# The last two output-gate units of the first mixer, computed as a pair of seven half-size products

## The chip, the cores and the metric

The kernel runs on one core of one Trainium2 chip. TensorE (PE) multiplies, VectorE (DVE), ScalarE (ACT) and GpSimd (POOL) work element by element, and SyncE (SP) and POOL issue DMA transfers. The metric is the device time of one execution in microseconds; the span is the time from the first instruction that the profile shows to the last.

## The reference, cut to what matters

A decoder block over 16 meta tokens and 512 tokens of width 1024, in float32. The normalised input is projected by one wide matrix; two token mixers (an mLSTM, "m", and gated linear attention, "g", four heads each) work on the projections, two branches are merged by sigmoid gates, and a SwiGLU layer follows.

```python
xn = rmsnorm(h, norm1_g[l])
proj = jnp.where(valid, xn @ w_in[l].astype(dt), 0.0).astype(dt)
(mq, mk, mv, mi, mf, mo, gq, gk, gv, ga, gr, gate_m, gate_g) = split_cols(proj)
...
hm = mlstm_chunkwise(...)
hm = head_rmsnorm(from_chunks(hm), m_head_g[l]) * jax.nn.sigmoid(mo.astype(f32)).reshape(bsz, tp, M_HEADS, M_DV)
y_m = hm.reshape(bsz, tp, M_V).astype(dt)
...
merged = (jax.nn.sigmoid(gate_m) * (y_m @ w_branch_m[l].astype(dt))
          + jax.nn.sigmoid(gate_g) * (y_g @ w_branch_g[l].astype(dt)))
h = h + merged @ w_out[l].astype(dt)
```

The change is in how `mo`, the output gates of the mLSTM, are computed for its last head.

## The kernel before, in words

**Units.** A projection is computed transposed, in units of 128 output features: eight blocks k of 128 input features, and for each block three matmuls, since every float32 operand is split into a high part and a low remainder (high x high, high x low, low x high; `mm3`, lines 340 to 347). A unit over the tokens alone is 24 matmuls of 512 columns (`unit_real`); one over all 528 positions is 48 of 264 (`unit_all`). Unit `mo i` gives 128 gate features; head h uses mo 2h and mo 2h+1, `mv` gives the values, `mq` and `mk` queries and keys.

**Pairs.** From the gm units on, two neighbouring units are computed together by a Strassen-like scheme (`pair`, line 397; `seven`, line 384): inputs and columns are halved, and seven products of half size (q1, p7, p3, q6, p4, p2, q5) take the place of eight. Each is four blocks k of three matmuls with 256 or 272 columns. The products share three PSUM banks: bx takes q1, then q6, q5 and p3; bz takes p7 and p4; by takes p2. Between them parts of the banks are copied out by ACT (`s1`, `s2`, `s5`, `s7`, `c12`, lines 475 to 480) and combined by DVE (`c11`, `c21`, `c22`). p3 of one pair, and its last combinations, are computed in the place for p3 of the next pair; the first pair finds that place empty, and takes q1 ahead of p7.

**Weights.** A raw weight tile of each unit arrives on SP's queue, several units ahead (`load_raw`). A plain unit's is split by a cast on ACT and a subtraction on DVE (`split_hi`, `split_lo`). A pair's two tiles are combined: the second gets a half of the first added by an accumulating DMA on POOL; two more halves are fetched as tile `wf` (`fetch_mix`, lines 233 to 245, one pair ahead); DVE adds two halves (`s2` at line 263, `s4` at line 275), and four sets are split: e, a, f and the half-size g. f's low part is made at the end of p7 (`f_lo`), g's parts in q6 and p4.

**Operands.** The first units work on the gained but not yet normalised input `xh`, `xl`, and their results are multiplied by `rstd` when they leave PSUM. `normed_x` (line 629) builds the normalised set block by block, and writes it and negated halves to DRAM (`X.pos`, `X.neg`); when it is done, later units use it and their results are copied out by ACT. `mixed_x` (line 651, once for each half of the blocks) then builds the operands of the seven products: those of p2 and p3 are slices of the normalised set, those of q5, p7, q6 and p4 are read from DRAM with accumulating DMAs on POOL and then split, and those of q1 are copied by SP into tiles of their own (line 707). `X.ready` counts finished halves, and the first pair starts when it is 2.

**Order.** No scheduler reorders anything: the order in which the program is written is the order in each engine's list, and each engine works through its own list, waiting on semaphores. The main list of jobs (`job_list`) gives the matmuls. Everything else is written as Python generators: `tick()` advances each one step, and `yield n` means that its next step comes n ticks later. A unit ticks after each of its eight blocks k, a pair after every second hook, 14 times in all, four of them (two ticks) in the place of p3 even if no p3 is there. The generators in `side` advance on every tick; of `mixers` (the `mlstm` and `gla` heads, in order) only the first one does, so a head begins on the tick after the one before it ended. A head's `mlstm` writes score matmuls (line 1023), its numerators (lines 1076 to 1080, two halves one or two ticks apart) and the denominator (lines 1083 and 1084) in between the matmuls of the units.

The units around the change are, in order: mq 3, mk 3, mv 6, mv 7, mo 6, mo 7, then the pairs gm 0/1 and gm 2/3, then the pairs of the second mixer. `conv_act` (line 838) is the activation of queries and keys, `gates_of` applies tanh to the gates, `head_out` normalises a head's result and multiplies in the gate, `some_parts` splits the first branch operands.

Of the kernel before, what the change touches and what calls it, by code (L numbers as in the profile page):

```python
# [54 lines left out]
def job_list():  # L55

    one = lambda *a: [(x,) for x in a]
    o = one(("gates", 0))
    for h in range(H):
        v, g = [("mv", 2 * h), ("mv", 2 * h + 1)], [("mo", 2 * h), ("mo", 2 * h + 1)]  # L60
        o += one(("mq", h), ("mk", h), *([g[0], *v, g[1]] if h == 0 else v + g))
    two = lambda n, i: [((n, 2 * i), (n, 2 * i + 1))]
    g = lambda h: [(("gq", h), ("gk", h))] + two("gv", h) + two("gr", h)
    bm = lambda i: one(("bm", 2 * i), ("bm", 2 * i + 1))
    bgs = [m for i in range(4) for m in (i, i + 4)]
    o += two("gm", 0) + two("gm", 1) + g(0) + two("gm", 2) + two("gm", 3)
    for i in range(4):
        o += bm(i)
    q, v, r = ([g(h)[i] for h in range(H)] for i in range(3))
    o += [q[1], v[1], q[2], r[1], v[2], q[3], v[3], r[2], r[3]]  # L70
    for i in range(4):
        o += two("gg", i)
    o += one(*(("bg", m) for m in bgs))
    for i in range(4):
        o += two("out", i)
    for m in range(FT):
        if m == 0:
            for i in range(len(GCHUNKS)):
                o += one(("fx", i))
        if m >= NG:  # L80
            o += [(("fg", m), ("fu", m))]
    for i in range(len(CHUNKS)):
        o += one(("down", i))
    return o
# [36 lines left out]
def hybrid_block(ctx: ExitStack, tc: tile.TileContext, xT, xr, wst, wdn, wgu, fg, par, con, out):  # L121
# [14 lines left out]
    def tt(dt=F32, n=NT, p=P):  # L136
        t = tpool.tile([P, TW], dt, tag="t", name=nm("t"))
        return t[:p, :n]
# [34 lines left out]
    def tick():  # L173
        for e in list(side):
            advance(side, e)
        if mixers:
            advance(mixers, mixers[0])
# [452 lines left out]
    def normed_x():  # L630

        nh, nl = [], []
        for k in range(KT):
            t = tt()
            V.scalar_tensor_tensor(t, xs[k], pr[:, C_N1 + k:C_N1 + k + 1], rstd, ALU.mult, ALU.mult)
            yield 4
            hi, lo = tt(F32R), tt(F32R)
            S.copy(hi, t)
            neg = tt(n=HA)
            act(neg, t[:, 256:] if k < 4 else t[:, :HA], AF.Copy, scale=-1.0)  # L640
            nc.sync.dma_start(X.pos[k // 2][k % 2], t)
            nc.sync.dma_start(X.neg[k // 2][k % 2], neg)
            yield 1
            V.tensor_tensor(lo, t, hi.bitcast(F32), ALU.subtract)
            nh.append(hi)
            nl.append(lo)
            yield 2
        X.h, X.l, X.scale = nh, nl, None

    def mixed_x(i):  # L650

        while X.scale is not None:
            yield 24
        h, l = X.h, X.l
        c1, c2 = slice(0, HA), slice(256, NT)
        if X.w is None:
            X.w = {n: ([None] * 4, [None] * 4) for n in SEVEN}
        ks = (2 * i, 2 * i + 1)
        for j in range(2):
            for k in ks:  # L660
                X.w["p2"][j][k] = (h, l)[j][k + 4][:, c1]
                X.w["p3"][j][k] = (h, l)[j][k + 4][:, c2]
        three = lambda a: a.rearrange("p (j n) -> p j n", j=2)
        mem = lambda t, c: t[:, :, c].rearrange("j p n -> p j n")

        def two(n, src, neg=False):
            hi, lo = tt(F32R, 2 * HA), tt(F32R, 2 * HA)
            if neg:
                act(hi, src, AF.Copy, scale=-1.0)
            else:  # L670
                S.copy(hi, src)
            yield 3
            if neg:
                V.scalar_tensor_tensor(lo, src, -1.0, hi.bitcast(F32), ALU.mult, ALU.subtract)
            else:
                V.tensor_tensor(lo, src, hi.bitcast(F32), ALU.subtract)
            for j in range(2):
                for k in ks:
                    X.w[n][j][k] = (hi, lo)[j][:, (k % 2) * HA:(k % 2 + 1) * HA]

        t1, t3 = tt(n=2 * HA), tt(n=2 * HA)
        plus = lambda t, m, c: G.dma_start(three(t), mem(m, c), accum_op=ALU.add)
        nc.sync.dma_start(three(t1), mem(X.pos[i], c1))
        nc.sync.dma_start(three(t3), mem(X.pos[i + 2], c2))
        yield 7
        plus(t1, X.neg[i], c1)
        plus(t3, X.neg[i], c1)
        yield 7
        yield from two("q5", t1)
        yield 1  # L690
        plus(t1, X.pos[i + 2], c2)
        yield from two("p7", t3)
        del t3
        yield 14
        yield from two("q6", t1, True)
        yield 2
        plus(t1, X.neg[i + 2], c1)
        yield 11
        yield from two("p4", t1)
        del t1  # L700
        while unit_ix[0] < UNITS.index(("mo", 7)):
            yield 1
        for j in range(2):
            t = tt(F32R, 2 * HA)
            for k in ks:
                c = slice((k % 2) * HA, (k % 2 + 1) * HA)
                nc.sync.dma_start(t[:, c].bitcast(F32), (h, l)[j][k][:, c1].bitcast(F32))
                X.w["q1"][j][k] = t[:, c]
            yield 5
        X.ready += 1  # L710

    def evac(o, ps):

# [9 lines left out]
    def evac_all(box, ps):  # L723
        t = tt()
        evac(t, ps)
        box.v = t
        yield 1

    def evac_real(box, ps):
        t = tt(n=NS)  # L730
# [114 lines left out]
    def conv_act(q, k, src):  # L845
        while src[0].v is None or src[1].v is None:
            yield 1
        yield 4
        for b, a in ((q, src[0].v), (k, src[1].v)):
            t = tt(n=a.shape[1])  # L850
            act(t, a, AF.Tanh, scale=0.5)
            V.scalar_tensor_tensor(a, t, 1.0, a, ALU.add, ALU.mult)
            del t
        yield 2
        for b, a in ((q, src[0].v), (k, src[1].v)):
            n = a.shape[1]
            hi, lo = tt(F32R, n), tt(F32R, n)
            act(hi, a, AF.Copy, scale=0.5)
            yield 3
            V.scalar_tensor_tensor(lo, a, 0.5, hi.bitcast(F32), ALU.mult, ALU.subtract)  # L860
            b.v = hi, lo, a
        src[0].v = src[1].v = None
# [108 lines left out]
    def part(y, k, j):  # L971

        if j == 0:
            hi = hpool[0].tile([P, NS], F32R, tag="h", name=nm("h")) if k < 6 and y is ym else tt(F32R, NS)
            S.copy(hi, y[k])  # L975
            y[k] = y[k], hi
        else:
            s, hi = y[k]
            lo = tt(F32R, NS)
            V.tensor_tensor(lo, s, hi.bitcast(F32), ALU.subtract)  # L980
            y[k] = hi, lo, True

    def some_parts(y, n):
        if y is ym:
            while y[7] is None:
                yield 5
            open_hpool()
        for k in range(n):
            while y[k] is None:
                yield 7  # L990
            part(y, k, 0)
            yield 3
            part(y, k, 1)
            yield 5

    def mlstm(h, q, k, v, gates, dst):
        while not gts.ready or q.v is None or k.v is None:
            yield 2
        (qh, ql, qf), (kh, kl, kf) = q.v, k.v
        nml, em = tt(n=NS), tt(n=NS)  # L1000
        for t, row in ((nml, 0), (em, 1)):
# [96 lines left out]
    def gla_decay(h, gq, gk, dk):  # L1098
# [14 lines left out]
        for a in range(2):  # L1113
            c = slice(a * HALF, (a + 1) * HALF)
            act(l[:, c], ps[a], AF.Abs, bias=b)
            act(z[:, c], ps[a], AF.Relu, scale=-1.0, bias=nb)
        yield 2
        act(l, l, AF.Exp, scale=-1.0)
        yield 2
        act(l, l, AF.Ln, bias=b_one)  # L1120
# [12 lines left out]
        yield 5  # L1133
        e1, e2 = tt(n=NS), tt()
        act(e2, b3, AF.Exp, scale=1.0 / TAU)
        yield 3
        act(e1, b3[:, NM:], AF.Exp, scale=-1.0 / TAU)
        act(ex[:, 2], b3[:, NM - 1:NT - CH:CH], AF.Exp, scale=-1.0 / TAU)
        while gq.v is None or gk.v is None:
# [7 lines left out]

    def gla(h, dk, v, gates, dst):
        while dk.v is None:
            yield 7  # L1150
        yield 10
        qd, ki, ex = dk.v
        pk = bank()
# [258 lines left out]
    for job in JOBS[2:]:  # L1412
# [3 lines left out]
        if what in ("bm", "bg") and i % 2 or len(job) == 2 or job in JOBS[3:8]:  # L1416
            next(sums, None)
        if len(job) == 2:
            if what == "gm" and i == 0:
                while X.ready < 2:  # L1420
                    tick()
                for k in range(4):
                    X.h[k] = X.l[k] = None
            if what in ("gq", "gv", "gr"):
                b = head("g", i if what == "gq" else i // 2)
            if what == "gq":
                pair(job, X.w, ALL, sink_of((b.q, b.k), False, True))
            elif what == "gv":
                pair(job, X.w, ALL, sink_of(b.vf, True, True))
            elif what == "gr":  # L1430
                pair(job, X.w, REAL, sink_of(b.gates, False, False, AF.Silu))
            else:
                if what == "gg" and i == 6:
                    run(some_parts(yg, 2))
                elif what == "gm" and i == 4:
                    run(some_parts(ym, 4))
                pair(job, X.w, REAL, sink_of({"gm": gm, "gg": gg}[what][i:i + 2], False, False, AF.Tanh))
# [660 lines left out]
```

## Time and profile before

| | before |
|---|---|
| median of 3 runs | 895.92 us (895.58 to 896.02) |
| the profiled execution | 895.85 us |
| its span | 894.1 us |
| PE busy | 883.3 us, 99% |
| DVE busy | 706.7 us, 79% |
| ACT busy | 582.8 us, 65% |
| POOL busy | 115.3 us, 13% |
| HBM | 170.30 MB read, 36.85 MB written |

A row of the timeline gives start and duration in microseconds, engine, line, operation, the tiles written and read, their shapes, the count where rows were merged, and in brackets the idle time before and what ended it. A row of the waits gives the waiting instruction, what it waited for, the microseconds in total, how often, and the longest. A table by windows gives for each stretch its length, each engine's busy time with the number of instructions, TensorE's granted clock, the busy share of the DMA engines and what they moved. A row of groups gives the count, busy time and mean nanoseconds. mo 6 and mo 7 run from 159.71 to 176.11 us, among parts of heads 2 and 3; the first gm pair starts at 176.11.

### The profile page before, as it was taken

What the parts mean: (1) busy time and instruction counts of PE and PEld (TensorE: products, weight loads), DVE (VectorE), ACT (ScalarE), POOL (GpSimd) and SP (SyncE); (2) the same over time, 40 slices, a digit from 0 to 9 for tenths busy, and PEclk for the clock granted to TensorE, in tenths of its full rate; (3) what the DMA queues carried; (4) which work ended last, traced back from release to release, by engine and by line L of the source; (5) the groups of instructions that cost most, each with busy time, mean ns of one, the idle gap of its engine ahead of it and who ended that gap; (6) DMA issues with size and microseconds to landing.
All of it is one profiled execution on the core that took longest, in us unless ns stands there. A gap on an engine that the chain in (4) does not pass through costs nothing. (4 is left out here: it accounts for less than half of the span.)

```text
span 894.1 us, 16395 instructions
## 1 busy us (share of the span) xinstructions
PE 883.3 (99%) x6281; PEld 829.6 (93%) x6281; DVE 706.7 (79%) x1102; ACT 582.8 (65%) x1027; POOL 115.3 (13%) x148
## 2 busy tenths in 40 slices
PE   9999999999999999999999999999999999999996
PEld 8999989889998899999998899999999999988885
DVE  4879776888765477687788899999777777798987
ACT  7677777798774276776876457765655555666564
POOL 0100031022211122221210111011111121000000
PEclk9999999999999999999999999999999999999999
DMA  9887585589985898988978776667877677456562
GB/s 342 269 241 208 155 171 124 162 246 226 247 218 146 210 225 244 251 214 218 227 187 244 198 170 171 210 191 169 198 179 208 178 169 193 122 191 198 179 199 105
DMA packets 67582, 178.93 MB, mean 200 GB/s; under 512 B 7432, under 2 KB 12680, under 8 KB 65072
## 3 DMA queue, kind: packets, MB, share of 16 engines
q1 hardware_dynamic: 50224, 137.07, 46.2%
q0 software_dynamic: 17136, 40.77, 27.7%
q8 instruction: 49, 0.80, 0.4%
q14 instruction: 29, 0.24, 0.1%
q10 hardware_dynamic: 144, 0.04, 0.0%
HBM read 170.30 MB, written 36.85 MB: 232 GB/s over the span
## 5 line engine op out<-in xcount | busy, mean ns | idle before, releaser
L392 PE MATMUL b<-t,whi 128*128 128x256 f32 (+1 forms) x1008 | 289.3, 287 | 2.7 <-ACT t L475 1.8
L226 DVE TENSOR_TENSOR wlo<-raw,whi 128x1024 fp32r<-128x1024 f32 x179 | 214.5, 1200 | 89.3 <-ACT whi L221 88.4
L394 PE MATMUL b<-t,wlo 128*128 128x256 f32 (+1 forms) x1008 | 284.3, 282 | 0.0
L393 PE MATMUL b<-t,whi 128*128 128x256 f32 (+1 forms) x1008 | 284.3, 282 | 0.0
L221 ACT CAST whi<-raw 128x1024 fp32r<-128x1024 f32 x179 | 184.8, 1034 | 42.2 <-PE b L346 9.9
L392 PEld LDWEIGHTS b<-t,whi 128*128 128x128 f32 x1008 | 190.1, 189 | 4.6 <-ACT t L475 2.4
L393 PEld LDWEIGHTS b<-t,whi 128*128 128x128 f32 x1008 | 190.2, 189 | 0.4
L394 PEld LDWEIGHTS b<-t,wlo 128*128 128x128 f32 x1008 | 189.8, 188 | 0.0
L346 PE MATMUL b<-t,whi 128*128 128x264 f32 (+2 forms) x448 | 148.0, 330 | 0.2 <-DVE t L980 0.2
L152 ACT ACTIVATE t<-t 128x512 f32<-128x512 f32 (+10 forms) x168 | 88.2, 539 | 83.8 <-DVE t L1689 39.5
L345 PE MATMUL b<-t,whi 128*128 128x264 f32 (+2 forms) x400 | 131.5, 329 | 0.0
L347 PE MATMUL b<-t,wlo 128*128 128x264 f32 (+2 forms) x400 | 129.5, 324 | 0.2 <-DVE wlo L561 0.2
L346 PEld LDWEIGHTS b<-t,whi 128*128 128x128 f32 x448 | 84.3, 188 | 8.4 <-DVE t L980 0.5
L209 POOL DMA_DIRECT2D raw<-wst x41 | 35.8, 873 | 383.3 <-DMA wf<-wst 108.9
L347 PEld LDWEIGHTS b<-t,wlo 128*128 128x128 f32 x400 | 75.2, 188 | 6.6 <-DVE wlo L561 0.4
L345 PEld LDWEIGHTS b<-t,whi 128*128 128x128 f32 x400 | 75.4, 188 | 6.2 <-ACT t L975 0.2
L1945 PE MATMUL b<-whi,t 128*128 128x512 f32 (+1 forms) x156 | 61.2, 392 | 0.0
L1944 PE MATMUL b<-wlo,t 128*128 128x512 f32 (+1 forms) x156 | 61.2, 392 | 0.0
L1943 PE MATMUL b<-whi,t 128*128 128x512 f32 (+1 forms) x156 | 60.7, 389 | 0.0
L221 ACT CAST whi<-wf 128x1024 fp32r<-128x1024 f32 x42 | 44.1, 1049 | 20.8 <-PE b L393 9.3
L245 POOL DMA_DIRECT2D wf<-wst x42 | 40.2, 963 | 131.4 <-DVE t L1718 35.6
L226 DVE TENSOR_TENSOR wlo<-wf,whi 128x1024 fp32r<-128x1024 f32 x42 | 51.1, 1218 | 0.0
(301 smaller groups left out, 1646.3 us busy)
## 6 DMA issues: line engine op xcount, KB each, us to landing
raw<-wst SPq DMA_DIRECT2D x123, 512.0 KB, 5.0
wf<-wst SPq DMA_DIRECT2D x42, 256.0 KB, 3.9
wf<-wst POOLq DMA_DIRECT2D x42, 256.0 KB, 6.2
raw<-wst POOLq DMA_DIRECT2D x41, 256.0 KB, 4.6
raw<-wdn SPq DMA_DIRECT2D x15, 512.0 KB, 3.7
sum_q<-wdn POOLq DMA_DIRECT2D x10, 512.0 KB, 9.1
sum_p<-wdn POOLq DMA_DIRECT2D x10, 512.0 KB, 9.0
raw<-sum_q SPq DMA_DIRECT2D x10, 512.0 KB, 4.1
```

The source lines that it names most:

```text
L152: S.activation(o, i, func, **kw)
L221: S.copy(t, src)
L226: V.tensor_tensor(t, src, hi.bitcast(F32), ALU.subtract)
L345: T.matmul(o, w_h, ah[:, c0:c1], start=first, stop=False)
L346: T.matmul(o, w_h, al[:, c0:c1], start=False, stop=False)
L347: T.matmul(o, w_l, ah[:, c0:c1], start=False, stop=last)
L392: T.matmul(o, h, xh_[k][:, c0:c1], start=start and k == 0, stop=False, skip_group_check=not start)
L393: T.matmul(o, h, xl_[k][:, c0:c1], start=False, stop=False, skip_group_check=not start)
L394: T.matmul(o, l, xh_[k][:, c0:c1], start=False, stop=k == 3, skip_group_check=not start)
L1943: T.matmul(o, hi, wh, start=n not in INTO and k == 0 or (i, k) == (1, FH - 2), stop=False, skip_group_check=True)
L1944: T.matmul(o, hi, wl, start=False, stop=False, skip_group_check=True)
L1945: T.matmul(o, lo, wh, start=False, stop=k == FH - 1, skip_group_check=True)
```

## The change

mo 6 and mo 7 become one job, `two("mo", 3)`, ahead of the gm pairs: the first pair of the kernel. Its sink applies tanh to the combined result as before. q1's operands are slices of the normalised set while that pair runs, and are copied into tiles of their own while it runs: one of the two `mixed_x` generators makes all four copies, from the first tick behind mv 7 on. The wait for `X.ready` stands ahead of every pair. The set `normed_x` takes ten ticks a block instead of seven. In `mixed_x` one step comes a tick sooner. Further steps get other tick counts: `conv_act`, `mlstm` (polls on every tick), `gla_decay`, `gla` and `some_parts`, which also skips a part that is already split; `evac_all` has another count at its very end.

```diff
@@ job_list
-        o += one(("mq", h), ("mk", h), *([g[0], *v, g[1]] if h == 0 else v + g))
+        o += one(("mq", h), ("mk", h), *([g[0], *v, g[1]] if h == 0 else v + g if h < 3 else v))
     two = lambda n, i: [((n, 2 * i), (n, 2 * i + 1))]
+    o += two("mo", 3)
@@ normed_x
             nc.sync.dma_start(X.neg[k // 2][k % 2], neg)
-            yield 1
+            yield 4
             V.tensor_tensor(lo, t, hi.bitcast(F32), ALU.subtract)
@@ mixed_x
                 X.w["p3"][j][k] = (h, l)[j][k + 4][:, c2]
+                X.w["q1"][j][k] = (h, l)[j][k][:, c1]
...
         plus(t3, X.neg[i], c1)
-        yield 7
+        yield 6
...
-        while unit_ix[0] < UNITS.index(("mo", 7)):
-            yield 1
-        for j in range(2):
-            t = tt(F32R, 2 * HA)
-            for k in ks:
-                c = slice((k % 2) * HA, (k % 2 + 1) * HA)
-                nc.sync.dma_start(t[:, c].bitcast(F32), (h, l)[j][k][:, c1].bitcast(F32))
-                X.w["q1"][j][k] = t[:, c]
-            yield 5
         X.ready += 1
+        if X.ready < 2:
+            return
+        while unit_ix[0] <= UNITS.index(("mv", 7)):
+            yield 1
+        for k in range(0, 4, 2):
+            for j in range(2):
+                t = tt(F32R, 2 * HA)
+                for m in range(2):
+                    c = slice(m * HA, (m + 1) * HA)
+                    nc.sync.dma_start(t[:, c].bitcast(F32), X.w["q1"][j][k + m].bitcast(F32))
+                    X.w["q1"][j][k + m] = t[:, c]
+                    (h, l)[j][k + m] = None
+                yield 2
@@ conv_act
-        yield 2
+        yield 3
         for b, a in ((q, src[0].v), (k, src[1].v)):
...
-            yield 3
+            yield 2
@@ mlstm
         while not gts.ready or q.v is None or k.v is None:
-            yield 2
+            yield 1
@@ gla_decay
-        yield 2
+        yield 1
         act(l, l, AF.Exp, scale=-1.0)
...
-        yield 3
+        yield 5
         act(e1, b3[:, NM:], AF.Exp, scale=-1.0 / TAU)
@@ gla
-            yield 7
+            yield 8
@@ some_parts
-            part(y, k, 0)
-            yield 3
-            part(y, k, 1)
+            if not isinstance(y[k], tuple):
+                part(y, k, 0)
+            yield 4
+            if len(y[k]) == 2:
+                part(y, k, 1)
@@ main loop, jobs of two units
-            if what == "gm" and i == 0:
-                while X.ready < 2:
-                    tick()
-                for k in range(4):
-                    X.h[k] = X.l[k] = None
+            while X.ready < 2:
+                tick()
...
+            elif what == "mo":
+                pair(job, X.w, REAL, sink_of(head("m", i // 2).gates, False, False, AF.Tanh))
```

More of the change, by code (lines that the diff above doesn't have):

```diff
@@ L700, in mixed_x @@
         del t1
-        while unit_ix[0] < UNITS.index(("mo", 7)):
+        X.ready += 1
+        if X.ready < 2:
+            return
+        while unit_ix[0] <= UNITS.index(("mv", 7)):
             yield 1
-        for j in range(2):
-            t = tt(F32R, 2 * HA)
-            for k in ks:
-                c = slice((k % 2) * HA, (k % 2 + 1) * HA)
-                nc.sync.dma_start(t[:, c].bitcast(F32), (h, l)[j][k][:, c1].bitcast(F32))
-                X.w["q1"][j][k] = t[:, c]
-            yield 5
-        X.ready += 1
+        for k in range(0, 4, 2):
[7 more added lines that the diff above has]
+                yield 2
     def evac(o, ps):
@@ L853, in conv_act @@
             del t
-        yield 2
+        yield 3
         for b, a in ((q, src[0].v), (k, src[1].v)):
```

## The prediction

> **What bounds the kernel now.** First the page, then the waits of TensorE, then busy time by stretch around the two units.
>
> ```profile
> span 894.1 us, 16395 instructions
> PE 883.3 (99%) x6281; PEld 829.6 (93%) x6281; DVE 706.7 (79%) x1102; ACT 582.8 (65%) x1027; POOL 115.3 (13%) x148
> ```
>
> ```profile
> PE b L392 <- ACT t L475: 1.8, 2, 1.4
> ...
> PE b L392 <- ACT t L476: 0.4, 1, 0.4
> ...
> ```
>
> ```profile
> core 0: us, PE busy (x) PEld busy (x) DVE busy (x) ACT busy (x) POOL busy (x), PEclk, DMA share, GB/s
> 100.00:146.70 46.70, 46.70 (x324) 43.79 (x323) 33.27 (x53) 35.26 (x73) 7.36 (x6) 1.00 0.61 151
> 146.70:159.71 13.01, 13.01 (x107) 12.93 (x106) 10.67 (x22) 10.30 (x21) 3.38 (x3) 1.00 0.56 105
> 159.71:176.11 16.40, 16.40 (x85) 13.87 (x84) 13.52 (x21) 10.59 (x18) 1.71 (x2) 1.00 0.76 209
> 176.11:187.07 10.96, 10.96 (x89) 10.74 (x87) 8.80 (x13) 10.55 (x24) 1.50 (x3) 1.00 0.66 241
> 187.07:199.66 12.59, 10.76 (x90) 10.46 (x89) 10.24 (x21) 10.97 (x22) 3.67 (x5) 1.00 0.92 210
> ```
>
> TensorE sets the time: it is idle for 10.8 us in all, at the granted clock 1.00 here. The last four stretches are mv 6 and mv 7; mo 6 and mo 7, the units that become a pair; the first gm pair; the second gm pair. Only the last has a hole, 1.83 us, and the waits name it: a product that must add to a bank waits until ScalarE has copied that bank out (lines 475 and 476). DVE and ACT are near their limit there, with 2.35 and 1.62 us idle. So the time moves by TensorE's instruction time, plus any new place where it waits for ACT or DVE, less the waits that go.
>
> **The products.** Two units are 2 x 8 x 3 = 48 matmuls of 512 columns; the pair is 7 x 4 x 3 = 84 of 256 columns. What counts is the step from start to start, since a matmul's duration overlaps the next one.
>
> ```profile
> 171.60 0.40 PE L345 MATMUL b<-t,whi 128*128 128x512 f32 x1
> ...
> 174.85 0.39 PE L347 MATMUL b<-t,wlo 128*128 128x512 f32 x1
> ```
>
> ```profile
> 195.10 0.28 PE L392 MATMUL b<-t,whi 128*128 128x256 f32 x1
> ...
> 197.44 0.28 PE L394 MATMUL b<-t,wlo 128*128 128x256 f32 x1
> ```
>
> The first two are 14 steps apart, 3.25 / 14 = 0.2321 us. The others are 20 apart, 2.34 / 20 = 0.1170. So 48 x 0.2321 = 11.14 us go and 84 x 0.1170 = 9.83 come: -1.31 us, all on the path, because TensorE has no hole there.
>
> A rule speaks against this. The Trainium skill (TensorE: Matmul & The Clock Gate, "Back-to-back issue gap") gives about 81 ns a matmul at 128 columns and 131 ns at 512 for a sustained stream with weight loads; an estimate between them for 256 is 98 ns, and by it the change would cost 84 x 98 - 48 x 131 ns = +1.9 us. This case's steps differ from it: 232 and 117 ns, so half the columns cost half the time.
>
> **The side work.** The raw weights of both units were split before (one cast, one subtraction each), and still are. The pair adds a third split of their sum and a fourth of half size, two sums, and the copying out of three banks by parts.
>
> ```profile
> L226 DVE TENSOR_TENSOR wlo<-wf,whi 128x1024 fp32r<-128x1024 f32 x2 | 2.4, 1216 | 0.0
> L295 DVE TENSOR_TENSOR wgl<-wg,wgh 128x512 fp32r<-128x512 f32 x2 | 1.4, 686 | 0.0
> L290 ACT CAST wgh<-wg 128x512 fp32r<-128x512 f32 x2 | 1.2, 623 | 0.0
> L221 ACT CAST whi<-wf 128x1024 fp32r<-128x1024 f32 x1 | 1.1, 1052 | 0.1
> L481 DVE SCALAR_TENSOR_TENSOR t<-b,t 128x256 f32<-128x256 f32 x2 | 0.8, 422 | 0.0
> L475 ACT COPY t<-b 128x256 f32<-128x256 f32 x2 | 0.7, 364 | 0.0
> ```
>
> DVE: 1.22 + 0.69 + two sums of 512 columns, at line 295's 0.69 each, + three combinations at 0.42 = 4.6 us. ACT: 1.05 + 0.62 + five copies at 0.36 = 3.5 us; the two tanh stay. Over 146.70 to 187.07 (40.37 us) the stretches show DVE idle 7.4 us and ACT 8.9 us, so it fits by volume and costs nothing by volume; without that cover it would cost up to 4.6 us. What can cost is its order.
>
> **The new pair's place.** It is the first pair, so no earlier product p3 is pending: q1 and p7 come, then q6 adds to q1's bank at once. q6 needs two late things: the bank copied out (line 475), and the low half of the summed weights, which DVE is told to make only at the end of p7. Each engine works through its own list in order.
>
> ```profile
> 159.71 0.39 PE L345 MATMUL b<-t,whi 128*128 128x512 f32 x1
> ...
> 162.49 0.49 PE L879 MATMUL b<-pr,t 128*128 128x128 f32 x3
> 162.73 0.48 PE L345 MATMUL b<-t,whi 128*128 128x512 f32 x1
> ...
> 164.21 0.40 PE L1078 MATMUL b<-wh,t 128*128 128x512 f32 x1
> ...
> 166.22 0.48 PE L345 MATMUL b<-t,whi 128*128 128x512 f32 x1
> ...
> 166.99 0.39 PE L1083 MATMUL b<-t,onesr 128*128 128x512 f32 x1
> ...
> 167.46 0.39 PE L345 MATMUL b<-t,whi 128*128 128x512 f32 x1
> ```
>
> ```profile
> 162.14 1.06 ACT L221 CAST whi<-raw 128x1024 fp32r<-128x1024 f32 x1
> 163.22 1.28 ACT L151 ACT_TABLE_LOAD   x1
> 164.52 1.17 ACT L152 ACTIVATE t<-t 128x512 f32<-128x512 f32 x2
> ```
>
> ```profile
> 163.50 0.68 DVE L1066 TENSOR_TENSOR t<-t,t 128x512 fp32r<-128x512 f32 x1
> 165.18 1.31 DVE L852 SCALAR_TENSOR_TENSOR t<-t,t 128x512 f32<-128x512 f32 x2 [1.00 <-ACT t L152]
> ```
>
> TensorE starts the pair at 159.71; q1 and p7 are 24 x 0.117 = 2.81 us, to 162.52; the transposes of the fourth tick 0.24, to 162.76. Head 2's numerator (2.01 us) and denominator (0.47) now stand on ticks 6 and 7. Head 0 polls every tick instead of every second one, starts a tick sooner, and each head starts when the one before it ends; so I take them on ticks 5 and 6, which in this pair lie in the empty place of p3, ahead of q6. That carries TensorE to 165.24, and the third matmul of q6 comes at 165.5.
>
> On ACT the cast of 162.14 belongs to the pair behind and slides back, so the table load and tanh end about 1.06 us sooner, at 164.6, and the bank is copied by 165.3 (two copies). That is about in time. On DVE the low half stands behind the two operations of line 852, which wait for that tanh: they would end at 166.49 - 1.06 = 165.4, and the subtraction (1.22) at 166.6. One more sum now stands ahead of them; if DVE and not the tanh is last (164.18 + 0.6), it is 167.3. The wait of q6 is so 1.1 to 1.8 us; I take 1.1, since head 2's earlier tick also moves its subtractions out of the way. Its ends: nothing, if both halves of the numerator come first; 167.7 - 162.8 = 4.9 us, if neither does and the tanh is as late as now.
>
> **The old waits.**
>
> ```profile
> 192.02 0.43 DVE L1036 TENSOR_TENSOR t<-b,t 128x272 f32<-128x272 f32 x1
> ...
> ```
>
> ```profile
> 192.49 0.42 ACT L1049 CAST wh<-t 128x272 fp32r<-128x272 f32 x1 [0.97 <-DVE t L1036]
> 192.81 0.37 ACT L475 COPY t<-b 128x256 f32<-128x256 f32 x1
> ```
>
> ```profile
> 193.23 0.38 PE L392 MATMUL b<-t,whi 128*128 128x256 f32 x1 [1.40 <-ACT t L475]
> ...
> 198.16 0.39 PE L392 MATMUL b<-t,whi 128*128 128x256 f32 x1 [0.44 <-ACT t L476]
> ```
>
> Behind the copy stands a cast for head 3, and behind that DVE. Head 3 and the gm pairs keep their places to each other (both come two ticks sooner: the pair has 14 ticks, the units had 16). But the new pair's p3, 12 x 0.117 = 1.40 us of TensorE, is done inside the first gm pair, whose extra work on DVE is one combination (0.42). So DVE has 1.0 us more to catch up. I take 1.0 of the 1.84 us back; the ends are 0 and 1.84.
>
> **What is moved.** The copy of q1's operands is eight SP transfers, now at 161.3 to 167.0:
>
> ```profile
> 161.31 5.71 SPq L707 DMA_DIRECT2D t<-t  x8
> ```
>
> ```profile
> pos<-t SPq DMA_DIRECT2D x5, 264.0 KB, 3.7
> t<-t SPq DMA_DIRECT2D x8, 136.0 KB, 3.3
> ```
>
> They are issued on ticks 1, 3, 5 and 7 of the pair, nearly the same moments, with the same weight loads of SP behind them; they land in 3.3 us and their reader, q1 of the gm pair, is over 8 us away. A pair's weights also need an accumulation on POOL and one more pair of quarter loads, at DMA shares of 0.56 to 0.76. All zero; if SP were held up, the weight loads behind would be, and they run units ahead.
>
> The normalised operands come 24 ticks later (ten ticks a block instead of seven). That puts six bank copies of mk 2, mv 4 and mv 5 on DVE instead of ACT, about 0.4 us each by line 481; DVE idles 13.4 us in 100 to 146.7. The mixed operands are read on the very tick on which the set is complete; its last write went out six ticks (some 4.2 us, at 3 x 0.2321 us a tick) before and lands in 3.7. If that is late, SP waits about a microsecond, then POOL's additions, then the split of q5, which has ticks to spare. Zero, with an end of +1. The other shifted ticks are zero with ends of -0.3 and +0.3.
>
> **Sum.** -1.31 + 1.1 - 1.0 = -1.2 us. The profiled execution took 895.85 us, 1.75 more than its span; the median is 895.92. So 894.7.
>
> **Rivals.** Each time is 895.92 plus the sum. A run here tells from no change only what is over 0.2%, 1.8 us.
>
> *Everything is covered* (0.24): both numerator halves or a prompt tanh come before q6, and the later waits close: -1.31 - 1.84 = -3.15, 892.8. For it: idle time on both engines, 7.4 and 8.9 us. Against: at 165.18 DVE still waits for the tanh.
>
> *Gain and waits cancel* (0.16): q6 waits 1.8 to 2.5 us and the second gm pair is no better: about +1.0, 896.9. For it: 4.6 us more on DVE.
>
> *A bare q6* (0.11), the slower one: head 2's numerator stays behind q6, so TensorE stands from 162.8 until the low half at 167.7. -1.31 + 4.9 = +3.6, 899.5. It decides from a wait of 3.1 us. Against: head 2 needs only one tick.
>
> *Elsewhere* (0.03): late operands, or half-size products dearer than half; 0.1326 us a step would already eat the gain, the row has 0.1170.
>
> **Numbers.** The forecast, 0.46, spans 893.9 to 895.7; about 0.08 of it is past 0.2%. Faster: 0.24 + 0.08 = 0.32. Same: 0.38 + 0.16 = 0.54. Slower: 0.14. The range reaches from everything covered, less the runs' 0.2, to the cancelling case with 0.4 on top: 892.6 to 897.3.
>
> **What would show it.** 48 fewer 512-column matmuls and 84 more of 256 at 0.117 us; a wait of TensorE on line 394 or 392 about 5 us into the pair, released by DVE's subtraction of the summed weights, near 1 us; the copies of lines 475 and 476 in the second gm pair down from 1.84 to about 0.8. It is wrong if the first wait passes 3 us, or if TensorE gets holes between 100 and 159.

## The result, and the profile after

| | before | after |
|---|---|---|
| median | 895.79 us (895.47 to 896.38, 12 runs) | 893.77 us (893.33 to 894.57, 12 runs) |
| ratio to before | 1 | 0.9978 [0.9969, 0.9987] |
| the profiled execution | 895.85 us | 893.4 us |
| its span | 894.1 us | 891.6 us |

The changed kernel is 2.0 us faster, just over the 0.2% that tells it from no change. The forecast was 894.7 us, 1.2 less than before; the time lies 0.9 us below it, inside the range. Lines have moved: the matmuls of a pair are 393 to 395 (were 392 to 394), the bank copies `s1`, `s2`, `s5`, `s7` are 476 to 479, and a subtraction for a low half is 227 (was 226).

The page of the changed kernel:

```profile
span 891.6 us, 16487 instructions
PE 881.7 (99%) x6317; PEld 830.1 (93%) x6317; DVE 711.4 (80%) x1115; ACT 583.8 (65%) x1028; POOL 117.4 (13%) x150
```

What TensorE waits for in it (total, times, longest):

```profile
PE b L393 <- ACT t L476: 0.9, 2, 0.5
PE b L393 <- ACT t L477: 0.4, 1, 0.4
```

The same stretches as before (length, busy time of PE, PEld, DVE, ACT, POOL with the number of instructions, granted clock, DMA share, GB/s):

```profile
core 0: us, PE busy (x) PEld busy (x) DVE busy (x) ACT busy (x) POOL busy (x), PEclk, DMA share, GB/s
100.00:146.70 46.70, 46.70 (x324) 43.80 (x323) 36.74 (x63) 33.42 (x68) 9.89 (x9) 1.00 0.69 166
146.70:159.71 13.01, 13.01 (x107) 12.92 (x106) 11.61 (x23) 11.27 (x23) 2.57 (x3) 1.00 1.01 227
159.71:176.11 16.40, 16.40 (x130) 15.92 (x129) 16.40 (x26) 13.80 (x25) 2.59 (x3) 1.00 0.72 169
176.11:187.07 10.96, 10.96 (x89) 10.75 (x88) 8.18 (x14) 10.39 (x25) 1.27 (x2) 1.00 0.85 303
187.07:199.66 12.59, 11.65 (x97) 11.35 (x96) 11.37 (x23) 11.75 (x23) 3.86 (x5) 1.00 0.98 252
```

TensorE has no hole up to 187 us: the new pair waits for almost nothing, though DVE has no idle moment in the pair's stretch (16.40 of 16.40 us). The stretches are those of before in time; the second gm pair now runs from 186.03 to 197.75, and its hole, in the last stretch, is 0.94 us, where it was 1.83. The DMA engines are full from 146.7 to 159.7, share 1.01 where it was 0.56.

TensorE around the new pair, and its two waits in the second gm pair:

```profile
159.72 0.28 PE L393 MATMUL b<-t,whi 128*128 128x256 f32 x1
...
162.52 0.49 PE L885 MATMUL b<-pr,t 128*128 128x128 f32 x3
162.76 0.48 PE L1086 MATMUL b<-wh,t 128*128 128x512 f32 x1
...
164.84 0.47 PE L1091 MATMUL b<-t,onesr 128*128 128x512 f32 x1
...
165.50 0.28 PE L394 MATMUL b<-t,whi 128*128 128x256 f32 x1
165.72 0.38 PE L395 MATMUL b<-t,wlo 128*128 128x256 f32 x1
...
191.30 0.39 PE L393 MATMUL b<-t,whi 128*128 128x256 f32 x1 [0.51 <-ACT t L476]
...
196.24 0.38 PE L393 MATMUL b<-t,whi 128*128 128x256 f32 x1 [0.43 <-ACT t L477]
```

The pair starts at 159.72; its first 24 products take 2.80 us, 0.1167 each. The third matmul of q6 comes 0.22 us behind the second instead of 0.117, and the next one, at 165.94, 0.22 behind the third: q6 waits 0.10 us and loses 0.2 in all. On ACT and DVE, what q6 needs:

```profile
159.59 0.62 ACT L1069 CAST t<-t 128x512 fp32r<-128x512 f32 x1 [1.24 <-DVE t L1065]
...
162.09 1.17 ACT L153 ACTIVATE t<-t 128x512 f32<-128x512 f32 x2
163.16 0.35 ACT L476 COPY t<-b 128x256 f32<-128x256 f32 x1
```

```profile
164.44 1.22 DVE L227 TENSOR_TENSOR wlo<-wf,whi 128x1024 fp32r<-128x1024 f32 x1
```

Tanh ends at 163.26, the bank is copied at 163.51, and the low half is ready at 165.66; the matmul that needs it starts at 165.72.

By terms: products -1.31, q6 +0.2, the second gm pair 0.94 instead of 1.83, -0.89: -2.0 us. The medians differ by 2.0 too, the two profiled executions by 2.45. The rest of the latter is not the change's: behind TensorE's last hole, at 478 us before and at 476 after, the kernel before takes 416.2 us to the end and the changed one 415.6, but e4 and e6 below, whose instructions there are the changed kernel's, take 416.1 and 416.2.

### The profile page after: what moved, and what is told of

Same layout as the page of the kernel before. It is cut to its first block, busy times and chain, and to the rows that moved or that the text cites. A ratio compares the mean times of both kernels' runs of the same rounds, so it can differ in the third digit from the quotient of the medians.

```text
span 891.6 us, 16487 instructions
## 1 busy us (share of the span) xinstructions
PE 881.7 (99%) x6317; PEld 830.1 (93%) x6317; DVE 711.4 (80%) x1115; ACT 583.8 (65%) x1028; POOL 117.4 (13%) x150
## 5 line engine op out<-in xcount | busy, mean ns | idle before, releaser
L393 PE MATMUL b<-t,whi 128*128 128x256 f32 (+1 forms) x1032 | 296.2, 287 | 1.8 <-ACT t L476 0.9
L394 PE MATMUL b<-t,whi 128*128 128x256 f32 (+1 forms) x1032 | 291.1, 282 | 0.0
L395 PE MATMUL b<-t,wlo 128*128 128x256 f32 (+1 forms) x1032 | 290.9, 282 | 0.0
L153 ACT ACTIVATE t<-t 128x512 f32<-128x512 f32 (+11 forms) x170 | 89.1, 540 | 88.7 <-DVE t L1696 39.8
L347 PE MATMUL b<-t,whi 128*128 128x264 f32 (+2 forms) x432 | 141.8, 328 | 0.2 <-DVE t L986 0.2
L346 PE MATMUL b<-t,whi 128*128 128x264 f32 (+2 forms) x384 | 125.2, 326 | 0.0
L348 PE MATMUL b<-t,wlo 128*128 128x264 f32 (+2 forms) x384 | 123.3, 321 | 0.2 <-DVE wlo L562 0.2
L246 POOL DMA_DIRECT2D wf<-wst x43 | 42.3, 989 | 130.5 <-DVE t L1725 35.5
```

Source lines behind the costliest of these rows:

```text
L153: S.activation(o, i, func, **kw)
L346: T.matmul(o, w_h, ah[:, c0:c1], start=first, stop=False)
L347: T.matmul(o, w_h, al[:, c0:c1], start=False, stop=False)
L348: T.matmul(o, w_l, ah[:, c0:c1], start=False, stop=last)
L393: T.matmul(o, h, xh_[k][:, c0:c1], start=start and k == 0, stop=False, skip_group_check=not start)
L394: T.matmul(o, h, xl_[k][:, c0:c1], start=False, stop=False, skip_group_check=not start)
```

## The experiments

The change has two parts that can be taken apart: the pair itself, and the tick counts of the generators. The first theory followed the prediction: the pair's shorter products and its p3 inside the first gm pair bring the time, and the tick counts are small. Its rival: the tick counts are what lets the pair run without waits. Every ratio and difference is to the kernel before, run beside it on the same chip; holes are stretches of over 50 ns in which TensorE does nothing, between 155 and 225 us of the profiled execution. A hole is counted from the end that the profile models for the matmul before it, so more is lost than its length: at e12's hole of 0.25 us (shown below) the matmul starts 0.53 us behind the one before and the next 0.23 behind that, where the step is 0.117. That is 0.27 us lost beyond the hole, and it is as much at the second hole of the second gm pair; where the number of holes differs, I count 0.27 for each, an estimate.

| | median us | less the median of before beside it | ratio | holes, us |
|---|---|---|---|---|
| before | 895.79 | 0 | 1 | 1.40 + 0.44 |
| changed | 893.77 | -2.0 | 0.9978 [0.9969, 0.9987] | 0.51 + 0.43 |
| e1, pair alone | 897.97 | +2.6 | 1.0032 [1.0020, 1.0045] | 2.41 + 0.45 + 1.54 + 0.17 + 0.69 |
| e2, ticks alone | 895.99 | +0.7 | 1.0006 [0.9998, 1.0015] | 0.26 + 0.15 + 0.52 + 1.22 |
| e3, poll of 2 | 900.79 | +5.1 | 1.0050 [1.0027, 1.0073] | 0.88 + 0.30 + 0.80 + 1.19 + 1.21 + 0.95 |
| e4, q1 copied first | 894.80 | -0.9 | 0.9989 [0.9977, 1.0000] | 0.20 + 0.29 + 0.34 + 0.50 + 0.43 |
| e5, numerator late | 897.77 | +2.4 | 1.0028 [1.0018, 1.0038] | 0.69 + 0.33 + 0.92 + 1.70 + 1.26 |
| e6, normalised set early | 894.16 | -1.6 | 0.9985 [0.9974, 0.9996] | 0.51 + 0.42 |
| e7, bank copies first | 893.00 | -2.3 | 0.9971 [0.9961, 0.9981] | 0.91 + 0.35 + 0.34 |
| e8, all in place | 892.75 | -3.1 | 0.9966 [0.9954, 0.9979] | 0.54 + 0.42 |
| e9, e7 and e8 | 891.77 | -4.1 | 0.9954 [0.9941, 0.9968] | 0.40 |
| e10, pair alone, in place | 899.13 | +3.2 | 1.0036 [1.0022, 1.0049] | 0.90 + 1.18 + 0.41 + 1.53 + 0.18 + 0.69 |
| e11, before, bank copies first | 894.57 | -0.7 | 0.9992 [0.9983, 1.0001] | 0.99 |
| e12, changed, again | 893.45 | -1.8 | 0.9978 [0.9969, 0.9987] | 0.25 + 0.50 + 0.42 |

**e1: the pair without the ticks.** The changed kernel with all ten changed counts set back.

```diff
@@ normed_x
-            yield 4
+            yield 1
@@ mixed_x
-        yield 6
+        yield 7
@@ evac_all, its end
-        yield 3
+        yield 1
@@ mlstm, the poll
-            yield 1
+            yield 2
...
```

> The pair and the moved copy of q1's operands, with every tick count as before the change. If the matmuls and the p3 in the first gm pair do the work (theory), the products give -1.31 us, the second gm pair waits about 0.94 us instead of 1.83 (-0.89), and only q6 of the new pair is later: head 2's numerator stands a tick later, so TensorE reaches q6 at about 164.8 us while DVE's subtraction of the summed weights ends after 166: a wait of 1 to 2 us. Sum -0.2 to -1.2 us, 894.6 to 895.6. If the tick counts are what relieves the second gm pair (rival), its waits stay near 1.8 us and the sum is 0 to +0.8 us, 895.8 to 896.6.

897.97 us, 2.6 more than before. TensorE's waits in it:

```profile
PE b L393 <- DMA t<-t: 2.4, 1, 2.4
PE b L393 <- ACT t L476: 1.7, 4, 0.7
PE b L393 <- ACT t L477: 1.5, 1, 1.5
```

The time is above the ranges of both. The holes sum to 5.26 us, 3.42 more than before; with 0.27 for each of three more holes, less the 1.31 of the products, that is +2.9. The medians differ by 2.6, the two profiled spans by 2.1 (896.2 and 894.1). Its first hole, 2.41 us, is q1 waiting for a transfer, which neither theory had. Its second gm pair waits 0.45 + 1.54 us, as much as before, although p3 lies inside the first gm pair here too. So p3's place alone does not bring the relief.

**e2: the ticks without the pair.** The same ten counts, put into the kernel before.

> The kernel before with the changed tick counts, the two units still plain. Theory: matmuls unchanged, and the second gm pair gets no p3 of an earlier pair in the first one, so its waits stay within 0.4 us of 1.83 us: 895.4 to 896.2. Rival (the tick counts relieve it): the waits fall to about 0.9 us and the time to about 894.9.

895.99 us; the interval spans no change. TensorE's waits:

```profile
PE b L392 <- ACT t L476: 1.4, 2, 1.2
...
PE b L394 <- DVE wlo L226: 0.5, 1, 0.5
```

The holes sum to 2.15 us, 0.3 more than before (0.8 with 0.27 for each of two more), but lie elsewhere: 0.26 us in the first gm pair, only 0.15 in the second, and 0.52 + 1.22 in the pair behind it. So the ticks do relieve the second gm pair, and without the new pair the wait comes back one pair later. If the parts added up, the changed kernel would stand at +2.6 + 0.7 = +3.3 us; it stands at -2.0. Some 5 us come only from both together, with 1 us or so of uncertainty in each part.

**e3: one tick count back.** The changed kernel with the `mlstm` heads polling on every second tick again.

```diff
         while not gts.ready or q.v is None or k.v is None:
-            yield 1
+            yield 2
```

> The changed kernel with the heads polling on every second tick again, and nothing else. Theory: heads 0 to 2 start one tick later, head 2's numerator stands on the pair's sixth tick and its denominator on the seventh, behind q6's first blocks; TensorE reaches q6 at about 164.8 us and DVE's subtractions are later by about a tick's work, ending at 166 to 167: a wait of 1 to 2 us, 894.4 to 895.6. Rival (the poll is of no account): the wait stays near 0.1 us and the time within 0.4 us of 893.8.

900.79 us (899.33 to 900.99, three runs), 5.1 more than before, so some 7 more than the changed kernel by the medians and 6.0 by the profiled spans (897.6 and 891.6). Neither range had that. ACT's row of the cast for head 2, and two of TensorE's:

```profile
163.43 0.62 ACT L1069 CAST t<-t 128x512 fp32r<-128x512 f32 x1 [3.35 <-DVE t L1065]
```

```profile
167.40 0.39 PE L393 MATMUL b<-t,whi 128*128 128x256 f32 x1 [0.80 <-ACT t L476]
...
169.09 0.39 PE L395 MATMUL b<-t,wlo 128*128 128x256 f32 x1 [1.19 <-DVE wlo L227]
```

The cast stands 3.84 us later than in the changed kernel (159.59), and ahead of the table load, the tanh and the bank copies in ACT's list; the bank copy is late by 3.83 us, the low half by 3.37, and q6 waits 1.99 us in two places, although the first half of head 2's numerator still stands ahead of it (164.36). How one tick becomes 3.84 us shows on DVE, in the operation that releases the cast, line 1065 on the last 16 columns, in the changed kernel and in e3:

```profile
159.34 0.17 DVE L1065 TENSOR_TENSOR t<-t,t 128x16 f32<-128x16 f32 x1
```

```profile
163.17 0.17 DVE L1065 TENSOR_TENSOR t<-t,t 128x16 f32<-128x16 f32 x1
```

The piece before it is late by 1.68 us already (157.57 and 155.89), and in e3 a weight sum (line 276, 0.68 us) and two operations of line 678 (1.35 us) stand ahead of the last piece in DVE's list, where in the changed kernel they stand behind it. The second gm pair waits 2.16. The holes explain 4.4 of the 6.0 us (5.33 less 0.94), and 5.5 with 0.27 for each of four more.

**e4: q1 never in place.** The eight transfers of q1's operands are made before the pair, as the kernel before makes them before its first pair.

```diff
-        while unit_ix[0] <= UNITS.index(("mv", 7)):
-            yield 1
         for k in range(0, 4, 2):
...
-                yield 2
```

> The changed kernel with q1's operands copied ahead of the new pair, all eight transfers at the end of mv 7, and not taken in place. At the rows' pace (597 ns an issue, 3.3 us to land) the last copies land at 160 to 163 us or later, where a free tile is late, while q1 wants its third block at 160.4. Theory (the place matters): q1 waits 0.5 to 3 us, 894.2 to 896.5. Rival: SP runs far enough ahead, no wait, 893.5 to 894.1.

894.80 us, 0.9 less than before, so it keeps less than half of the gain by the medians, though its interval overlaps the changed kernel's: q1 waits for transfers three times, 0.83 us.

**e5: the numerators of head 2 two ticks later**, so that q6 stands ahead of them.

```diff
-        yield 5
+        yield 7 if h == 2 else 5
```

> The changed kernel with head 2's numerators and denominator two ticks later, so that they stand behind q6 of the new pair instead of in the empty place of p3. Theory (they are the cover): TensorE reaches q6 at about 162.8 us, the copy of q1's bank ends at about 163.5 and DVE's subtraction at about 165.7, so it waits about 2.9 us there, and some of it comes back at the second gm pair's 0.94 us: 895.7 to 896.7. Rival (the tanh's earlier end alone makes q6 prompt): under 0.5 us of wait and 893.8 to 894.3.

897.77 us, 2.4 more than before. TensorE in q6, and the low half on DVE:

```profile
163.73 0.36 PE L393 MATMUL b<-t,whi 128*128 128x256 f32 x1
165.12 0.39 PE L395 MATMUL b<-t,wlo 128*128 128x256 f32 x1 [0.92 <-DVE wlo L227]
```

```profile
163.85 1.22 DVE L227 TENSOR_TENSOR wlo<-wf,whi 128x1024 fp32r<-128x1024 f32 x1
```

The wait of q6 is there, released by the low half, but 0.92 us: the low half ends at 165.07 and not at the 167.7 that I feared, and q1 had come a microsecond late, waiting 0.69 + 0.33 us. The loss is mostly elsewhere: the second gm pair waits 1.70 + 1.26 us, 2.0 more than in the changed kernel. Head 3 starts when head 2 ends, so it comes two ticks later, which I take for the cause; it was not tried apart. The numerator that moved cost more two pairs later than where it moved.

**e6: the normalised set at its old speed** (ten ticks a block back to seven).

```diff
             nc.sync.dma_start(X.neg[k // 2][k % 2], neg)
-            yield 4
+            yield 1
```

> The changed kernel with the normalised set at seven ticks a block as before the change. Theory: it is off the path, since TensorE has no hole between 100 and 159 us either way; the time stays within 0.4 us of 893.8. Rival (the slower set frees DVE ahead of the pair): DVE is later at 157 to 165 us, q6 waits 0.5 to 1.5 us and the time is 894.3 to 895.3.

894.16 us, 1.6 less than before, where the changed kernel is 2.0 less; the intervals overlap and the holes are the same. This count lies off the path, as costed.

**e7: the bank copy ahead of head 3's cast**, in the second gm pair alone; the tanh that the pair before it left over is put behind `s2`.

```diff
+        if names[0] == ("gm", 2):
+            mine["q1", 3], mine["p3", 0] = ["s1"], ["s7"]
+            todo["p4", 1] = todo.pop(("q6", 2))
```

> The changed kernel; in the second gm pair alone, ScalarE copies q1's bank right behind q1 and not behind two more ticks' work, and the tanh of the first gm pair (with its table load) goes behind the copy of q6's bank. If the two remaining waits of 0.51 and 0.43 us are only a matter of ScalarE's order, as read from its rows, both go: -0.9 us, 892.9. If DVE's lateness is behind them, they come back at a later product: 893.6 to 894.0.

893.00 us. The second gm pair has no hole any more, so what was left there came from ACT's order; 0.34 us stand in the pair behind it. But a new hole stands in q1 of the new pair:

```profile
160.38 0.35 PE L393 MATMUL b<-t,whi 128*128 128x256 f32 x1 [0.91 <-ACT t L728]
161.08 0.39 PE L394 MATMUL b<-t,whi 128*128 128x256 f32 x1 [0.35 <-DMA t<-t]
```

The edit does nothing there. The first row names a copy on ACT, but in the changed kernel the same copy ran after the pair had begun and nothing waited for it; the second names the transfer. This profile is of the slowest of e7's eight executions (893.70; the fastest took 891.80), so the usual wait may be shorter. The next two runs put it to the test.

**e8: q1 truly in place.** No copy of q1's operands goes out until the pair has begun.

```diff
-        while unit_ix[0] <= UNITS.index(("mv", 7)):
+        while unit_ix[0] <= UNITS.index(("mo", 6)):
```

> The changed kernel with all of q1's operands in place: no copy starts before the new pair has begun. In the changed kernel's trace the first three copies land at 158.70 to 159.42 us and the pair starts at 159.72; in another kernel of the same order they land at 160.67 to 161.35 and q1 waits 1.26 us. Theory (the copies are a race that some executions lose): the wait can't come up, the median falls by 0.2 to 0.6 us against the changed kernel's 893.8 and the runs lie closer together. Rival (the profiled execution without a wait is the usual one): 893.6 to 894.0.

**e9: e7 and e8 together.**

> All of q1's operands in place, and in the second gm pair ScalarE's copies first as in the earlier run, which measured 893.0 us with 1.26 us lost at q1 in its profile. Theory (the two are independent): 0.5 to 1.3 us below that, 891.8 to 892.5. Rival (the wait at q1 had given ACT and DVE the time by which the second gm pair was prompt): a wait of 0.5 us or more comes back there, 892.6 to 893.2.

e8 takes 892.75 us (892.54 to 893.23), e9 891.77 (891.63 to 892.15). Neither has a wait in q1. e8 gained more than its theory said, and not all of it is explained: in its profile 31.57 us lie between the start of the pair and the first wait's end in the second gm pair (159.29 to 190.86), and 31.58 in the first profile of the changed kernel (159.72 to 191.30), which had no wait in q1 either. What TensorE still waits for in e9 between 155 and 225 us, and its stretches of the second gm pair and of the pair behind it:

```profile
PE b L395 <- DVE wlo L227: 0.4, 1, 0.4
```

```profile
185.82:196.11 10.29, 10.29 (x91) 10.29 (x90) 9.24 (x18) 10.23 (x22) 1.37 (x2) 1.00 0.99 234
196.11:212.06 15.95, 15.55 (x117) 14.99 (x115) 13.18 (x22) 15.15 (x28) 5.97 (x8) 1.00 0.86 212
```

The second gm pair is without a hole, and one of 0.40 us is left between 155 and 225 us, in the pair behind it, for a low half. e9 beats the kernel before by 4.1 us and so the changed kernel by about 2; the intervals of e9 and of the changed kernel don't meet, those of e8 and of the changed kernel do.

**e10: the pair alone, with q1 truly in place** (e1 and e8). If the transfer were all that e1 lost, this would be 2.4 us faster than e1.

> The pair with every tick count as before the change, and all of q1's operands in place. The pair with the old tick counts measured 897.97 us and waited 2.41 us for a copy of q1. Theory (that wait was the early copy's alone): it goes, 895.4 to 896.0, and the waits of 0.45, 1.54 and 0.86 us behind it stay. Rival (with the old tick counts another thing is late as well, such as the copy of q1's bank or the summed weights): q6 waits over 1 us in its place, 896.5 to 897.8.

899.13 us, 3.2 more than before: no faster than e1. The rival held in what it said of q6; the time is above its range too.

```profile
PE b L393 <- ACT t L476: 2.5, 5, 0.9
...
PE b L395 <- DVE wlo L227: 1.2, 1, 1.2
```

The pair begins at once, and q6 waits 0.90 us for the bank and 1.18 us for the low half instead. e1's late start had hidden that: with the old ticks the cast for head 2 comes at 161.4 us in both, 1.8 us later than in the changed kernel.

**e11: the edit of e7 in the kernel before.**

> The kernel before, its two units still plain and its tick counts its own, with the second gm pair's copies on ScalarE put first as in the runs above. Theory (the waits of 1.40 and 0.44 us there are ScalarE's order, and need no pair to go): 894.2 to 894.9. Rival (DVE is as late as ScalarE and brings the wait back at the summed weights or at a later copy): 895.2 to 895.9.

894.57 us, 0.7 less than the kernel before beside it (895.29), in the theory's range, though the interval just holds 1. Its profile shows what went and what came:

```profile
PE b L394 <- DVE wlo L226: 1.0, 1, 1.0
```

The waits for the bank copies in the second gm pair, 1.84 us, are gone, and the pair behind it waits 1.0 us for a low half, on DVE. DVE seems to have used TensorE's wait in the one to be ready for the next; that was not tried apart.

**e12: the changed kernel once more**, for another profile of q1.

> The changed kernel once more, unaltered, beside the others. Theory (the early copies of q1 are a race): another execution's profile shows a wait of q1 on a copy of 0.1 to 1.3 us, or copies that land within 0.5 us of the pair's start, and the median stays 0.6 to 1.3 us above the 892.75 of all-in-place. Rival: no wait, copies that land over a microsecond early, and a median below 893.2.

893.45 us. SP's issue of the first four transfers, and q1:

```profile
152.75 3.31 SPq L713 DMA_DIRECT2D t<-t  x4
```

```profile
159.45 0.28 PE L393 MATMUL b<-t,whi 128*128 128x256 f32 x1
159.98 0.39 PE L394 MATMUL b<-t,whi 128*128 128x256 f32 x1 [0.25 <-DMA t<-t]
```

The unaltered kernel has a hole of 0.25 us here, where its first profile has none. The transfers go out at 152.75, while TensorE is still in mv 6. The three whose landing the trace has land at 159.54 to 160.27, and the pair begins at 159.45; in the first profile they land at 158.70 to 159.42, and it begins at 159.72. Whether q1 waits is a race between them.

## Why the prediction was right, and where it was not

**The products: right.** 48 matmuls of 512 columns fewer and 84 of 256 more, by the groups, of which one matmul of each triple is shown (after, then before):

```profile
L393 PE MATMUL b<-t,whi 128*128 128x256 f32 x840 | 239.8, 285 | 1.3 <-ACT t L476 0.5 <-ACT t L477 0.4
...
L347 PE MATMUL b<-t,whi 128*128 128x512 f32 x176 | 69.4, 394 | 0.2 <-DVE t L986 0.2
```

```profile
L392 PE MATMUL b<-t,whi 128*128 128x256 f32 x816 | 232.6, 285 | 2.2 <-ACT t L475 1.4 <-ACT t L476 0.4
...
L346 PE MATMUL b<-t,whi 128*128 128x512 f32 x192 | 75.6, 394 | 0.2 <-DVE t L980 0.2
```

816 became 840 (and 136 became 140 for the half-size weights g), 28 more; 192 of 512 columns became 176, 16 fewer. Three times that makes 84 and 48. The step of 0.117 us held in the new pair (0.1167). By the estimate that the prediction made from the Trainium skill's "Back-to-back issue gap" (TensorE: Matmul & The Clock Gate) the products would have cost 1.9 us more; the trace does not agree, since 0.1167 us is half of the 0.2321 at 512 columns.

**The side work by volume: right.** From 146.70 to 187.07 DVE works 36.19 us instead of 32.99, ACT 35.46 instead of 31.44, and TensorE has no hole there.

**The place of the numerator: right.** Transposes at 162.52, numerator at 162.76, ahead of q6; the forecast had 162.52 and 162.76.

**The wait of q6: the term that was mis-sized.** 1.1 us was forecast, 0.10 measured, 0.2 with the late step behind it. That is nearly all of the 0.9 us by which the forecast was off. The step that failed is "the table load and tanh end about 1.06 us sooner, at 164.6": they ended at 163.26, 2.43 sooner than before. I let only the weight cast slide out of ACT's way. ACT's row of head 2's cast in the kernel before, which I didn't use:

```profile
161.07 0.62 ACT L1061 CAST t<-t 128x512 fp32r<-128x512 f32 x1 [2.15 <-DVE t L1057]
```

ACT stands idle for 2.15 us there, waiting for head 2. Head 2's earlier tick, which I used to place the numerator on TensorE, also brings forward the cast that stands ahead of the tanh, from 161.07 to 159.59, and with it all that is queued behind. I counted the tick for TensorE, and for DVE's subtractions, but not for ACT. e3 shows that it matters: with the poll alone taken back the cast comes 3.84 us later and q6 waits 1.99 us.

**The old waits: right in size (-0.89 for -1.0) by luck, wrong in reason.** The place of p3 was said to give DVE 1.0 us to catch up. e1 and e10 have that place too, and their second gm pair waits 1.99 and 1.94 us. The relief comes with the ticks: e2, which has them alone, waits 0.15 us there, and pays in the next pair (1.74 us), which in the changed kernel it doesn't. In the changed kernel TensorE comes to that wait 1.04 us sooner than before and the copy that releases it 1.93 us sooner:

```profile
190.88 0.37 ACT L476 COPY t<-b 128x256 f32<-128x256 f32 x1
```

It was at 192.81 in the kernel before. DVE did catch up, but the rows give another reason than p3. In the kernel before DVE stood idle for 1.13 us, until ACT made the copy `s5` (line 477) at 189.19, behind a table load; in the changed kernel ACT makes it ahead of the load, and DVE does not wait:

```profile
189.57 0.43 DVE L483 SCALAR_TENSOR_TENSOR t<-t,t 128x256 f32<-128x256 f32 x1 [1.13 <-ACT t L477]
```

```profile
186.23 0.37 ACT L478 COPY t<-b 128x256 f32<-128x256 f32 x1
```

e7 shows that what is left, 0.94 us, is ACT's order. Which of the ticks bring the 1.93 us is settled only for the poll: with it alone taken back (e3) these holes are 2.16 us. The other counts were not tried one by one, but for e6's.

**The copies of q1: wrong.** They were said to go out on ticks 1, 3, 5 and 7 of the pair, and the description of the change says "from the first tick behind mv 7 on". Both are wrong: the unit counter is already past mv 7 while mv 7 runs, so the loop never waits, and the first four transfers go out 6.7 us before the pair:

```profile
153.03 3.31 SPq L713 DMA_DIRECT2D t<-t  x4
```

So q1's first two blocks read copies, and only the last two are read in place. "All zero" did not hold either: the holes are 0 and 0.25 us in two profiles of the changed kernel, 1.26 in e7, 2.41 in e1.

**"The other shifted ticks are zero with ends of -0.3 and +0.3": wrong,** and the worst of the steps. With the pair and the other nine counts in place, the poll alone is worth 6 to 7 us (e3); all ten taken back cost 4.6 (e1, +2.6 against -2.0). That the forecast came out near is in part luck: what the ticks and the pair do only together was put down to the pair. I had seen the poll's effect in one place and costed the rest of it at nothing.

**The rivals.** *A bare q6* was made in e5, with the numerators behind q6, and its price was too high: 0.92 us of wait, not 4.9, because the low half ends at 165.07 and not at 167.7, and because q1's own wait had used up a microsecond. Nor is a numerator ahead of q6 enough by itself: in e10 it is ahead, at 162.22, and q6 waits 2.08 us, since there the cast and the tanh are late. *Everything is covered* came closest of the rivals: q6 is covered, and half of the later waits stayed. *Gain and waits cancel* did not occur. *Elsewhere* named late operands: q1's copies are such, with no wait in one profile of the changed kernel and 0.25 us in the other. With that row of the cast the sum would have been a microsecond lower, -2.2, and *faster* the likeliest case instead of one of 0.32.

**What would show it.** Of the four signs, the counts and the second gm pair's waits (0.94 for 0.8) came as said, and there is no hole from 100 to 159; the wait of 1 us in q6 did not come.

## What to carry to other kernels

When each engine works through a written list, a tick count that moves one step moves everything queued behind it on every engine: cost it on all of them, and expect that two edits, each worth nothing or a loss alone, may together be worth several microseconds. A wait removed uncovered the next one that it hid twice here (e10, e11), so price the second-latest need as well. And when operands are read in place to save a copy, read off the trace when the copy is issued, not off the condition in the code.

## What the runs showed of the hardware

The landing time of the same transfers differs between runs that move the same bytes. The page's row of the copies of q1 (KB each, median us to landing), in the changed kernel, in e8, and in e7:

```profile
t<-t SPq DMA_DIRECT2D x8, 136.0 KB, 4.5
```

```profile
t<-t SPq DMA_DIRECT2D x8, 136.0 KB, 3.5
```

```profile
t<-t SPq DMA_DIRECT2D x8, 136.0 KB, 5.3
```

It was 3.3 before, which I had taken over unaltered, and 4.9 in e12. In the changed kernel the first four go out in a stretch in which the DMA engines are full:

```profile
153.00:158.00 5.00, 5.00 (x43) 5.00 (x42) 4.36 (x10) 5.00 (x11) 0.00 (x0) 1.00 1.00 284
```

The share is 1.00 in these five microseconds of the changed kernel, and 0.66 in the seven that follow. In e7 and e12 it is 0.90 in the five microseconds from the issue on, and in e8, from 160 to 166 us, where its first four go out, 0.56. So the copies land later where the engines are busier, but not in step: e7's land later than the changed kernel's at a lower share. That the load is the cause is not shown; no run changed the load alone.
